# A Strassen-stepped attention block: first head pair by plain block products, last output block row by row, side transfers on another queue

## The chip, the cores and the metric

The kernel runs on one core of a Trainium2 chip. TensorE (PE) multiplies, VectorE (DVE) and ScalarE (ACT) work on tiles in SBUF and PSUM, GpSimd (POOL) does small things, and SyncE (SP) issues most DMAs. Each engine works through its own list of instructions in order. The metric is the device time of one launch in microseconds, lower is better.

## The reference

One layer is computed (DEPTH is 1, so only the neighbourhood attention of the two mixers), on 512 tokens of width 2048:

```python
h = rms_norm(x, norm_pre)
q, k, v, z = split(h @ na_w_in, 4)            # 2048 -> 4 * 2048
o = neighbourhood_attention(q, k, v, na_rpb)  # 16 heads of 128, 8 x 16 windows on an 8 x 64 grid
y = (o * silu(z)) @ na_w_out                  # 2048 -> 2048
out = x + rms_norm(y, norm_post)
```

The norm of a row of `h` is a factor per token, so the kernel multiplies the unnormalised `x` (scaled by the gain of each column) with the weights and applies the factor `rc` to the product.

## The kernel before, in words

**Products.** Every float32 operand is cut into a high part (`hi`, rounded to the fast matmul type by a CAST on ACT) and the rest (`lo`, a subtraction on DVE); a product is then three matmuls, hi by hi, lo by hi and hi by lo. One matmul is 128 x 128 by 128 x 512.

**Input steps.** The input product runs in `NSTEP` = 8 steps, one for each pair of heads. A step multiplies a 512 x 2048 activation with 2048 x 1024 weights. Both are cut in two along each dimension (blocks A11 to A22, B11 to B22), and a Strassen-Winograd scheme with seven block products (`NPASS`) replaces the eight plain ones. A pass is `KH` = 8 slots of k, a slot six matmuls (`mm_in`), so a step is 56 slots (`SLOTS`), 336 matmuls. The passes need sums of blocks. Sums of weights are made in the running tiles `T` on DVE (line 209) from `T` and a raw tile; sums of the activation are the same in all steps, are made once in the first step (`prep_a`, lines 129 to 151: A11, S1, A12, N2, A22, N4, N3), cut into hi and lo, and kept in SBUF as tiles `a`. So in the first step ACT and DVE have, beside the weights' work, the scaling of `x` by the gain (line 121), the sums (137 to 148) and the cuts (126, 127), one operand a slot. `combine` adds the passes' results into the four quadrants of the product.

**Beside the first step.** `square_x` loads `x` again in token order, 16 tiles `sq` of 256 KB in two alternating buffers, and ACT squares and sums them (line 166). After the last, `rstd` makes `rc` (DVE twice, then `pow` on POOL, line 171). Mask and squares are placed by slot number (`at`).

**Look-ahead.** `prep(m)` cuts the weights of slot m two slots ahead of the matmuls (`AHEAD`); `hi` and `lo` have three buffers each, raw weights four (`NRAW`). A framework lays tiles out in the pools, sets the waits, and sets the final order in each engine's list, close to the order of the code.

**Heads.** While step s runs, the attention of step s-1's two heads is laid beside its slots by the table `HEAD`. `load_bias` loads a head's position table, `keep_g` writes its gated output to DRAM (`graw`), `fetch_g`/`split_g` read it back (`gr`) and cut it into hi and lo (lines 486, 487) in the space of `a` tiles no longer used. All of these DMAs are issued on SP's list, between the loads of weights.

**Output.** Four blocks n of 512 output columns, each 16 slots of k; a slot multiplies four row tiles t of 128 tokens, twelve matmuls (`mm_out`). In each block the last two slots run tile by tile, so `finish(n, t)` can begin on tile 0 while PE is on tile 1. For the last block `finish` squares and sums (ACT, line 589), forms the row's norm (DVE 594, POOL 595), multiplies by the gain (DVE 596), scales four quarter rows and adds `x` (three on DVE, line 604; one on ACT and POOL, 601 and 602), and writes them out (606). `load_res` loads the residual tiles `xres`.

## Time and profile before

| | |
|---|---|
| median of 3 runs | 933.33 us (931.19 to 935.33) |
| the profiled execution | 932.95 us |
| its span, first to last instruction | 931.2 us |
| PE busy | 885.5 us, 95% |
| DVE, ACT busy | 730.5 us, 557.9 us |
| DMA | 180.1 MB, 193 GB/s over the span |

Times inside the profile count from the start of the span; the execution is 1.75 us longer than its span. PE's busy time counts overlapping matmuls whose ends are modelled, so a busy PE may still run below its pace; the pace is read from the distance of their starts. The times at which each step's first matmul starts cut the span into stages.

### The profile page before, as it was taken

The page shows a single profiled execution, that of the slowest core. Times are in us where ns is not written, and L with a number is a line of the kernel's source. Part 1 is how long each engine was busy: PE and PEld are TensorE (multiplying, and loading weights), DVE is VectorE, ACT ScalarE, POOL GpSimd, SP SyncE. Part 2 cuts the span into 40 slices and gives each one's busy share as a digit, 9 for nine tenths or more (in the row PEclk, how much of TensorE's full clock was granted, in tenths as well). Part 3 has the DMA queues.
Part 4 walks back from the last instruction along what each step waited for, and adds up shares of the span by engine and source line. Part 5 has one row for each costly group of instructions (what it writes and reads, how often), then busy time and mean ns, then how long its engine had stood idle before and what let it go on. Part 6 is the DMA issues. An engine that isn't in the chain of part 4 may idle for free.

```text
span 931.2 us, 13211 instructions
## 1 busy us (share of the span) xinstructions
PE 885.5 (95%) x4176; PEld 726.3 (78%) x4176; DVE 730.5 (78%) x1370; ACT 557.9 (60%) x1119; POOL 12.3 (1%) x18
## 2 busy tenths in 40 slices
PE   7887999999999999999999999999989999999992
PEld 6565788888788888888888888788868778888882
DVE  6997989897989799899979897989799654232326
ACT  8985675575658575766675575658566563232322
POOL 0000000000000000000000000000000000000003
PEclk9999999999999999999999999999999999999997
DMA  9798657865684678377656765685589922333325
GB/s 311 218 282 260 178 156 226 253 196 157 209 258 151 207 222 255 110 230 227 218 140 219 243 206 155 207 267 179 173 254 306 266 81 86 95 101 92 101 58 181
DMA packets 101734, 180.11 MB, mean 193 GB/s; under 512 B 11552, under 2 KB 17696, under 8 KB 101664
## 3 DMA queue, kind: packets, MB, share of 16 engines
q1 hardware_dynamic: 101232, 178.75, 62.6%
q8 instruction: 32, 0.52, 0.2%
q10 hardware_dynamic: 432, 0.53, 0.2%
q14 instruction: 38, 0.31, 0.1%
HBM read 171.37 MB, written 7.86 MB: 192 GB/s over the span
## 4 chain that ended last, share of the span: by engine, by line
issue 89%; DMA 5%; DVE 2%; ACT 1%; POOL 1%; PE 1%; SPq 0%; DVEq 0%; POOLq 0%; ACTq 0%
DMA sq<-in_x 2%; DMA x<-in_xT 1%; DMA raw<-in_w_in 1%; DVE lo L214 1%; PE u0Y L243 1%; POOL xres L602 1%; DVE a L127 1%; ACT hi L213 1%; DVE t L209 0%; DVE xres L604 0%; POOL rc L171 0%; ACT yg L601 0%; POOL rcy L595 0%; DVE x L141 0%; ACT a L126 0%
## 5 line engine op out<-in xcount | busy, mean ns | idle before, releaser
L213 ACT CAST hi<-t 128x512 fp32r<-128x512 f32 x320 | 196.1, 617 | 119.7 <-DVE t L209 25.0
L214 DVE TENSOR_TENSOR lo<-raw,hi 128x512 fp32r<-128x512 f32 x192 | 131.2, 690 | 135.3 <-ACT hi L213 129.0
L214 DVE TENSOR_TENSOR lo<-t,hi 128x512 fp32r<-128x512 f32 x320 | 217.4, 685 | 16.5 <-ACT hi L213 14.8
L213 ACT CAST hi<-raw 128x512 fp32r<-128x512 f32 x192 | 118.7, 621 | 152.6 <-PE y L583 93.3
L209 DVE TENSOR_TENSOR t<-t,raw 128x512 f32<-128x512 f32 x256 | 171.8, 686 | 14.3 <-DMA raw<-in_w_in 13.2
L583 PE MATMUL y<-hi,g 128*128 128x512 f32 x512 | 159.3, 392 | 0.4 <-DVE e L291 0.4
L583 PEld LDWEIGHTS y<-hi,g 128*128 128x128 f32 x512 | 95.1, 188 | 21.2 <-DVE e L291 0.9
L583 PE MATMUL y<-lo,g 128*128 128x512 f32 x256 | 99.7, 390 | 0.0
L583 PEld LDWEIGHTS y<-lo,g 128*128 128x128 f32 x256 | 48.1, 188 | 9.9
L243 PE MATMUL u0Y<-hi,a 128*128 128x512 f32 x96 | 27.8, 401 | 5.0 <-ACT a L126 2.6
L369 DVE TENSOR_TENSOR bm<-braw,mask_sb 128x256 f32<-128x256 f32 x48 | 27.2, 597 | 0.0
L243 PE MATMUL u1Y<-hi,a 128*128 128x512 f32 x96 | 26.8, 396 | 0.0
L243 PE MATMUL u2Y<-hi,a 128*128 128x512 f32 x96 | 26.8, 396 | 0.0
L243 PE MATMUL u3Y<-hi,a 128*128 128x512 f32 x96 | 26.8, 396 | 0.0
L243 PE MATMUL u4Y<-hi,a 128*128 128x512 f32 x96 | 26.8, 396 | 0.0
L243 PE MATMUL u6Y<-hi,a 128*128 128x512 f32 x96 | 26.8, 396 | 0.0
L243 PE MATMUL u5Y<-hi,a 128*128 128x512 f32 x96 | 26.8, 396 | 0.0
L243 PE MATMUL u7Y<-hi,a 128*128 128x512 f32 x96 | 26.8, 395 | 0.0
L298 ACT ACTIVATE s<-s,rc 128x512 f32<-128x512 f32 x32 | 22.9, 719 | 6.2 <-DVE s L283 5.7
L243 PE MATMUL u0X<-hi,a 128*128 128x512 f32 x64 | 19.7, 427 | 7.2 <-ACT hi L213 7.2
L243 PEld LDWEIGHTS u0Y<-hi,a 128*128 128x128 f32 x96 | 17.1, 188 | 12.0 <-ACT a L126 3.6
L243 PE MATMUL u0Z<-hi,a 128*128 128x512 f32 x64 | 18.4, 407 | 6.9 <-ACT hi L213 6.8
(405 smaller groups left out, 1858.5 us busy)
## 6 DMA issues: line engine op xcount, KB each, us to landing
raw<-in_w_in SPq DMA_DIRECT2D x384, 256.0 KB, 3.5
t<-in_w_in SPq DMA_DIRECT2D x128, 256.0 KB, 3.2
raw<-in_w_out SPq DMA_DIRECT2D x64, 256.0 KB, 2.6
x<-in_xT SPq DMA_DIRECT2D x32, 128.0 KB, 3.9
xres<-in_x SPq DMA_DIRECT2D x16, 256.0 KB, 6.9
graw<-zm SPq DMA_DIRECT2D x14, 256.0 KB
gr<-graw SPq DMA_DIRECT2D x14, 256.0 KB, 3.9
out<-xres SPq DMA_DIRECT2D x14, 256.0 KB, 3.0
```

Source lines behind the costliest of these rows:

```text
L127: nc.vector.tensor_tensor(lo, src, hi.bitcast(F32), ALU.subtract)
L209: nc.vector.tensor_tensor(T[k], T[k], src, ALU.add)
L213: nc.scalar.copy(hi, src)
L214: nc.vector.tensor_tensor(lo, src, hi.bitcast(F32), ALU.subtract)
L243: nc.tensor.matmul(U[c][s], l, r, start=p in (0, 1, 4) and k == 0 and s not in seen, stop=k == KH - 1 and n in (2, 5), skip_group_check=True,)
L298: nc.scalar.activation(t[:, s, :], t[:, s, :], AF.Copy, scale=rc[:, j + s : j + s + 1])
L369: nc.vector.tensor_tensor(bm[:, i, :].rearrange("p (a b) -> p a b", b=8), rev, mask_sb[:, i, :].unsqueeze(2).to_broadcast([P, 32, 8]), ALU ...
L583: nc.tensor.matmul(Y[n][t], l[:, tsl], r, start=k == 0 and i == 0, stop=k == KT - 1 and i == 2)
L602: nc.gpsimd.tensor_tensor(r, yg[q, t], r, ALU.add)
```

## The change

**First step.** Its seven passes become two (n = 0, 1) of 16 slots each (`FIRST` = 32 slots). Pass n forms one column half of the product by the plain sum over k: in a slot, four row tiles by one weight tile, twelve matmuls (`mm_first`), into four PSUM banks. No sums of weights are made, no `combine`; `take_first` copies the banks out with `rc` applied, for pass 0 from slot 22 on, for pass 1 at the end. An x tile is loaded whole (256 KB instead of two halves), scaled whole and cut whole (`take_x`): A11 and A12 go to their own place, A21 and A22 for now to the places of N4 and beside A12. The sums for later steps (`sum_x`) and their cuts lie at slots 12 to 25. The squares come one in every slot of twelve matmuls from slot 2 (before: one in every second slot of six, from slot 10), `rstd` at slot 20.

**Side transfers.** Mask, `load_bias`, `keep_g` and `fetch_g` are issued from GpSimd's list. The fetches move: heads 0 to 7 from slot 30 of the last input step, every third slot, into the space of A12 and A22; heads 8 to 13 one a slot from the first output slot. The residual tiles lie in the space of N2 and N3.

**Last block.** The last `TAIL` = 6 slots of the last block run tile by tile instead of 2; their weight cuts get buffers of their own (`w_tiles`). The last block's `y` lies in `T`.

```diff
+FIRST = 2 * KT
+TAIL = 6
...
+    AT = {}
+    for k in range(KH):
+        for n, ops in enumerate(((A11, N4, S1), (A12, A22), (N2, N3))):
+            t = ag.tile([P, len(ops), 2, 256], F32R, tag=f"a{k}_{n}", name=f"a{k}_{n}")
+            for i, o in enumerate(ops):
+                AT[k, o] = (t, i)
+
+    def A(k, o):
+        t, i = AT[k, o]
+        return t[:, i]
...
+    def load_x(k):
+        kk = k % KH
+        if k >= KH:
+            X[k] = small("v" if kk < 4 else "z", f"x{k}")
+        elif kk < 4:
+            X[k] = small("qk", f"x{k}")
+        else:
+            if kk % 2 == 0:
+                X["c", kk] = pair(f"x{k}")
+            X[k] = X["c", kk - kk % 2][:, kk % 2, :]
+        nc.sync.dma_start(X[k], xT[k])
+
+    def split_a(k, src, o):
+
+        t, i = AT[k, o]
+        src = src.rearrange("p (a b) -> p a b", b=256)
+        hi, lo = t[:, i : i + 2, 0, :], t[:, i : i + 2, 1, :]
         nc.scalar.copy(hi, src)
         nc.vector.tensor_tensor(lo, src, hi.bitcast(F32), ALU.subtract)
 
-    def prep_a(o, k):
-        x0, x1 = (X.get(k), X.get(k + KH))
+    def take_x(k):
+        nc.scalar.activation(X[k], X[k], AF.Copy, scale=gcol[:, k : k + 1])
+        split_a(k % KH, X[k], A11 if k < KH else A12)
...
+    def sum_x(k):
+        nc.vector.tensor_tensor(x1[:, h1], x0[:, h1], x1[:, h1], ALU.subtract)
+        nc.vector.tensor_tensor(x0[:, h1], x0[:, h0], x0[:, h1], ALU.subtract)
+        nc.vector.tensor_tensor(x0[:, h0], x0[:, h0], x1[:, h1], ALU.subtract)
+        nc.vector.tensor_tensor(x1[:, h0], x1[:, h0], x0[:, h0], ALU.subtract)
...
-    NIN = NSTEP * SLOTS
+    NIN = FIRST + (NSTEP - 1) * SLOTS
     NOUT = 4 * KT
     N = NIN + NOUT
 
+    def base(step):
+        return FIRST + (step - 1) * SLOTS if step else 0
...
+    def w_tiles(m):
+        if m < N - TAIL:
+            return tuple(wp.tile([P, L], F32R, tag=t, name=f"{t}{m}") for t in ("hi", "lo"))
+        i = m - N + TAIL
+        return tuple(small(("qk", "v", "z")[i // 2], f"{t}{m}", F32R) for t in ("hi", "lo"))
+
     def prep(m):
-        if m < NIN:
-            step, p, k = where(m)
-            if step == 0:
-                prep_a(p, k)
+        sums = FIRST <= m < NIN and where(m)[1] in (1, 3, 4, 6)
+        if m < FIRST and where(m)[1] == 0:
+            take_x(m)
...
+            if p == 1 and k >= KH:
+                load_t(1, B11, k - KH)
...
+    def mm_first(m):
+        _, n, k = where(m)
+        if k == 0:
+            if n == 0:
+                U[n] = [pm.tile([P, L], F32, tag=f"u{j}", name=f"u0_{j}") for j in range(4)]
+            else:
+                U[n] = [px.tile([P, L], F32, tag="ST"[j // 2], name=f"u1_{j}") for j in range(4)]
+        hi, lo = W.pop(m)
+        kk = k % KH
+        a = (A(kk, A11), A(kk, N4)) if k < KH else (A(kk, A12), A(kk, A22))
+        ops = [
+            (a[j // 2][:, i, j % 2 * P : j % 2 * P + P], w, j, i2)
+            for i2, (i, w) in enumerate(((0, hi), (1, hi), (0, lo)))
+            for j in range(4)
+        ]
+        if k == KT - 1:
+            ops.sort(key=lambda op: op[2])
+        for l, r, j, i in ops:
+            nc.tensor.matmul(U[n][j], l, r, start=k == 0 and i == 0, stop=k == KT - 1 and i == 2)
+
+    def take_first(n, j):
+        c = C.setdefault(0, {})
+        name = ("11", "12", "21", "22")[n + j // 2 * 2]
+        if j % 2 == 0:
+            c[name] = pair(f"c{name}_0")
+        nc.scalar.activation(c[name][:, j % 2, :], U[n][j], AF.Copy, scale=rc[:, j : j + 1])
...
-        nc.sync.dma_start(raw[:, 0 : 7 * TBL + 32], src)
+        nc.gpsimd.dma_start(raw[:, 0 : 7 * TBL + 32], src)
...
-            nc.sync.dma_start(graw[h], z_of[h])
+            nc.gpsimd.dma_start(graw[h], z_of[h])
...
-            nc.sync.dma_start(g, graw[h])
+            nc.gpsimd.dma_start(g, graw[h])
...
+            t = ag.tile([P, 2, L], F32R, tag=f"a{k}_{1 - o}", name=f"g{h}")
...
-            m = NIN - SLOTS + 17 + 3 * h if h < HEADS - 4 else NIN + h - HEADS + 4
+            m, wait = (NIN - SLOTS + 30 + 3 * h, 4) if h < KH else (NIN + h - KH, 3)
             at(m, fetch_g, h)
-            at(m + 4, lambda h=h: done.pop(h)())
+            at(m + wait, lambda h=h: done.pop(h)())
...
-        at(10 + 2 * i, begin)
-        at(14 + 2 * i, lambda i=i: pending.pop(i)())
-    at(45, rstd)
-    at(40, lambda: nc.sync.dma_start(mask_sb, mask))
+        at(2 + i, begin, i)
+        at(4 + i, lambda i=i: pending.pop(i)())
+    at(8, lambda: nc.gpsimd.dma_start(mask_sb, mask))
+    at(20, rstd)
+    for j in range(4):
+        at(22 + j, take_first, 0, j)
+        at(FIRST - 1, take_first, 1, j)
+    for k in range(KH):
+        at(KT - 4 + k, sum_x, k)
+        at(KT - 3 + k, lambda k=k: split_a(k, X[k], N2))
+        at(KT + 1 + k, lambda k=k: split_a(k, X[k + KH], N4))
...
+            free[k] = ag.tile([P, 2, L], F32, tag=f"a{k}_2", name=f"spare{k}")
...
-        y = yg[n, t] = spare(16 + n * 4 + t, f"yg{n}_{t}") if n < 2 else pair_half(n * 4 + t)
+        y = yg[n, t] = pair_half(n * 4 + t) if n < 3 else T[4 + t]
...
+        if 0 <= m and m + 3 < KT:
+            load_x(m + 3)
...
+            last = TAIL if n == 3 else 2
+            if k < KT - last:
                 mm_out(m, range(4))
             elif k == KT - 1:
                 for t in range(4):
-                    mm_out(m - 1, [t])
-                    mm_out(m, [t])
+                    for mm in range(m - last + 1, m + 1):
+                        mm_out(mm, [t])
                     finish(n, t)
```

**ACT, first step.** Names: `sq` the squares' tiles, `hi` weights, `a` and `x` the activation, `c` a copy out of PSUM. Before, around the fifth square:

```order
L166 ACTIVATE sq_548,part<-sq_548 128x512
L213 CAST hi_625<-raw_559 128x512
L126 CAST a_3_150<-x_190 128x256
L126 CAST a_3_157<-x_190 128x256
L126 CAST a_4_123<-x_257 128x256
L126 CAST a_4_130<-x_275 128x256
L166 ACTIVATE sq_584,part<-sq_584 128x512
L213 CAST hi_641<-t_161 128x512
```

and now, in the first pass, around the sixth:

```order
L164 ACTIVATE sq_351,part<-sq_351 128x512
L140 ACTIVATE x_362<-x_362,gcol 128x512
L164 ACTIVATE sq_377,part<-sq_377 128x512
L136 CAST a_1_112<-x_362 128x2x256
L227 CAST hi_382<-raw_281 128x512
L140 ACTIVATE x_388<-x_388,gcol 128x512
L164 ACTIVATE sq_403,part<-sq_403 128x512
L136 CAST a_1_115<-x_388 128x2x256
L227 CAST hi_409<-raw_307 128x512
```

A slot now has a scaling, a cut of `x`, a cut of a weight and a square, in that company four ACT instructions of 512 columns for twelve matmuls. Where the scale factor arrives, after the last square, ACT now has:

```order
L164 ACTIVATE sq_621,part<-sq_621 128x512
L164 ACTIVATE sq_648,part<-sq_648 128x512
L227 CAST hi_598<-raw_491 128x512
L271 ACTIVATE c_0_776<-u_0_184,rc 128x512
L271 ACTIVATE c_0_776<-u_1_185,rc 128x512
L227 CAST hi_629<-raw_521 128x512
```

Here `hi_598` is the weight of slot 18 and `hi_629` that of slot 19, which now stands behind two copies that read `rc`.

**SP and POOL, last input step.** Before, on SP (`gr` a fetched head, `xres` a residual tile, `t` and `raw` weights):

```order
L100 DMA t_163<-in_w_in 128x512
L610 DMA xres_0_8901<-in_x 128x1x512
L478 DMA gr_7643<-graw 128x512
L100 DMA t_164<-in_w_in 128x512
L478 DMA gr_7694<-graw 128x512
L100 DMA t_165<-in_w_in 128x512
L610 DMA xres_1_8903<-in_x 128x1x512
L100 DMA t_166<-in_w_in 128x512
L198 DMA raw_7651<-in_w_in 128x512
L198 DMA raw_7672<-in_w_in 128x512
L100 DMA t_167<-in_w_in 128x512
```

Now SP has only weights there, and POOL's list holds the fetches, a bias table and the write of head 13:

```order
L514 DMA gr_7521<-graw 128x512
L514 DMA gr_7586<-graw 128x512
L514 DMA gr_7633<-graw 128x512
L514 DMA gr_7726<-graw 128x512
L504 DMA graw<-zm_7222 128x512
L399 DMA braw_7945<-in_rpb 128x1x368
L514 DMA gr_7780<-graw 128x512
L514 DMA gr_7823<-graw 128x512
L514 DMA gr_7853<-graw 128x512
L514 DMA gr_7884<-graw 128x512
```

The fetches no longer stand between weights; nine are ahead of the write of head 13, five behind it.

**PE, last block.** Before, the two last slots (`hi_9397`, `hi_9413`) by tiles `y_0`, `y_1`, after `y_3` of the slot ahead:

```order
L583 MATMUL y_3_9189<-lo_9382,g_0_8200 128x512
L583 MATMUL y_0_9186<-hi_9397,g_0_8266 128x512
L583 MATMUL y_0_9186<-hi_9397,g_1_8267 128x512
L583 MATMUL y_0_9186<-lo_9398,g_0_8266 128x512
L583 MATMUL y_0_9186<-hi_9413,g_0_8486 128x512
L583 MATMUL y_0_9186<-hi_9413,g_1_8487 128x512
L583 MATMUL y_0_9186<-lo_9414,g_0_8486 128x512
L583 MATMUL y_1_9187<-hi_9397,g_0_8266 128x512
```

and now, six slots:

```order
L629 MATMUL y_3_8898<-lo_9021,g_7881 128x512
L629 MATMUL y_0_8895<-hi_9038,g_7913 128x512 x2
L629 MATMUL y_0_8895<-lo_9039,g_7913 128x512
L629 MATMUL y_0_8895<-hi_9056,g_7948 128x512 x2
L629 MATMUL y_0_8895<-lo_9057,g_7948 128x512
L629 MATMUL y_0_8895<-hi_9074,g_7983 128x512 x2
L629 MATMUL y_0_8895<-lo_9075,g_7983 128x512
L629 MATMUL y_0_8895<-hi_9078,g_8044 128x512 x2
L629 MATMUL y_0_8895<-lo_9079,g_8044 128x512
L629 MATMUL y_0_8895<-hi_9082,g_7986 128x512 x2
L629 MATMUL y_0_8895<-hi_9086,g_8208 128x512 x2
L629 MATMUL y_1_8896<-hi_9038,g_7913 128x512 x2
```

Between the last matmul of one row tile and that of the next there are now 18 matmuls instead of 6; the number of matmuls is the same.

## Rows read from the trace of the kernel before

**Rows 1.** Busy time by stretch: first pass of the first step, its rest, the fourth step, the last input step, the output blocks, the end. Columns: stretch in us, its length, busy us (instructions) of PE, PEld, DVE, ACT, POOL, granted clock of PE as a share, share of DMA time, GB/s.

```profile
0.00:20.10 20.10, 15.39 (x64) 13.02 (x65) 12.40 (x24) 16.44 (x36) 0.91 (x9) 1.00 0.92 309
20.10:107.00 86.90, 72.59 (x294) 52.15 (x294) 80.30 (x168) 65.86 (x157) 2.26 (x1) 1.00 0.87 253
281.90:368.70 86.80, 86.80 (x425) 72.72 (x424) 78.06 (x146) 57.02 (x111) 0.00 (x0) 1.00 0.67 210
631.50:725.70 94.20, 89.29 (x426) 72.11 (x425) 83.51 (x157) 62.63 (x123) 0.00 (x0) 1.00 0.74 228
725.70:914.10 188.40, 186.36 (x857) 153.04 (x855) 73.56 (x138) 68.41 (x141) 2.23 (x2) 1.00 0.36 103
914.10:931.20 17.10, 0.00 (x0) 0.00 (x0) 12.04 (x16) 2.74 (x5) 6.92 (x7) 0.62 0.77 241
```

**Rows 2.** The matmul line's groups (ns min/median/max of one, first and last start in us): the first chain of steps 0 and 1, and the output product.

```profile
L243 PE MATMUL u0X<-hi,a x64: 387/389/796, 4.7 to 47.7; 128*128 128x512 f32 x64
L243 PE MATMUL u1X<-hi,a x64: 387/393/477, 107.0 to 142.7; 128*128 128x512 f32 x64
L583 PE MATMUL y<-hi,g x512: 387/389/499, 725.7 to 913.4; 128*128 128x512 f32 x171
```

**Rows 3.** Timeline of PE (start us, us, what): two successive slots of six matmuls at full pace, and the warm-up products in the first step with the matmul behind them.

```profile
159.90 1.07 PE L243 MATMUL u1Z<-hi,a 128*128 128x512 f32 x4
161.26 1.07 PE L243 MATMUL u1Z<-hi,a 128*128 128x512 f32 x4
...
8.71 2.72 PE L83 MATMUL warm<-ident 128*128 128x128 f32 x16
11.19 0.48 PE L243 MATMUL u0X<-hi,a 128*128 128x512 f32 x1
```

**Rows 4.** Groups by line of the first 110 us, ACT and then DVE: busy us, mean ns of one, idle before.

```profile
L213 ACT CAST hi<-t 128x512 fp32r<-128x512 f32 x44 | 26.8, 615 | 10.7 <-DVE t L209 5.8 <-PE u0Z L243 2.4 <-PE u0X L243 0.9
L126 ACT CAST a<-x 128x256 fp32r<-128x256 f32 x48 | 18.1, 400 | 0.7 <-DVE x L148 0.3
L121 ACT ACTIVATE x<-x,gcol 128x256 f32<-128x256 f32 x32 | 15.6, 505 | 0.7 <-DMA gcol<-in_gpre 0.7
L166 ACT ACTIVATE sq<-sq 128x512 f32<-128x512 f32 x16 | 10.1, 631 | 4.7 <-DMA sq<-in_x 4.5
L166 ACT ACTIVATION_READ_ACCUMULATOR sq<-sq 128x1 f32 x16 | 3.0, 186 | 0.0
L298 ACT ACTIVATE s<-s,rc 128x512 f32<-128x512 f32 x4 | 2.9, 719 | 0.7 <-DVE s L283 0.7
...
L209 DVE TENSOR_TENSOR t<-t,raw 128x512 f32<-128x512 f32 x32 | 21.9, 686 | 0.5 <-DMA raw<-in_w_in 0.4
L127 DVE TENSOR_TENSOR a<-x,a 128x256 fp32r<-128x256 f32 x48 | 19.5, 421 | 5.9 <-ACT a L126 5.9
```

**Rows 5.** DMA: the mean rate in 10 to 20 us, then, of 49.3 to 63 us, the mean rate and the issues of the squares' tiles (KB each, median us from issue to landing); the same row of the whole page; and ACT's timeline of two successive squares, with the idle time before each and what ended it.

```profile
DMA packets 3036, 3.66 MB, mean 366 GB/s; under 512 B 335, under 2 KB 2160, under 8 KB 3036
...
DMA packets 2164, 3.94 MB, mean 288 GB/s; under 512 B 239, under 2 KB 239, under 8 KB 2164
sq<-in_x SPq DMA_DIRECT2D x5, 256.0 KB, 4.4
...
sq<-in_x SPq DMA_DIRECT2D x12, 256.0 KB, 5.6
...
58.90 0.63 ACT L166 ACTIVATE sq<-sq 128x512 f32<-128x512 f32 x1 [0.16 <-DMA sq<-in_x]
61.46 0.63 ACT L166 ACTIVATE sq<-sq 128x512 f32<-128x512 f32 x1 [0.19 <-DMA sq<-in_x]
```

**Rows 6.** Timeline where the row factor `rc` is made and first used.

```profile
88.89 2.26 POOL L171 TENSOR_TENSOR rc<-ms,mhalf 128x4 f32<-128x4 f32 x1 [87.43 <-DVE ms L170]
...
91.19 0.72 ACT L298 ACTIVATE c<-c,rc 128x512 f32<-128x512 f32 x1 [3.44 <-POOL rc L171]
```

**Rows 7.** Timeline of the end: the first row tile's square, the last matmul, the starts of row tiles 2 and 3 on DVE, and DVE's last group (three instructions).

```profile
910.02 0.60 ACT L589 ACTIVATE yg<-y 128x512 f32<-128x512 f32 x1 [3.68 <-PE y L583]
911.61 3.11 DVE L604 SCALAR_TENSOR_TENSOR xres<-yg,rcy,xres 128x512 f32<-128x512 f32 x3
913.68 0.39 PE L583 MATMUL y<-lo,g 128*128 128x512 f32 x1
918.51 0.20 DVE L594 TENSOR_SCALAR msy<-part,ms 128x1 f32<-128x1 f32 x1
922.38 0.20 DVE L594 TENSOR_SCALAR msy<-part,ms 128x1 f32<-128x1 f32 x1
923.24 3.08 DVE L604 SCALAR_TENSOR_TENSOR xres<-yg,rcy,xres 128x512 f32<-128x512 f32 x3
```

**Rows 8.** The last input step, 631.5 to 725.7 us: what ACT's cut of the fetched heads waited for (us in total, times, longest), and the DMA issues (KB each, median us to landing).

```profile
ACT g L486 <- DMA gr<-graw: 8.1, 9, 1.8
...
gr<-graw SPq DMA_DIRECT2D x13, 256.0 KB, 3.9
...
xres<-in_x SPq DMA_DIRECT2D x6, 256.0 KB, 7.3
```

**Rows 9.** Two lines' instructions (ns min/median/max): DVE's scale-and-add of the end, two inputs from SBUF, and POOL's addition that runs beside some of them.

```profile
L604 DVE SCALAR_TENSOR_TENSOR xres<-yg,rcy,xres x12: 744/752/1776, 911.6 to 924.6; 128x512 f32<-128x512 f32 x12
...
L602 POOL TENSOR_TENSOR xres<-yg,xres x4: 1737/1737/1759, 912.4 to 924.0; 128x512 f32<-128x512 f32 x4
```

129 lines of the change are left out of this document (43 added, 86 removed).

## The prediction

> **What bounds the kernel now.** I read the stretches first, to see where PE is busy but not at its pace. In a middle step PE is busy for all of 86.80 us [rows 1], so this stage is PE's own time. Its pace is read from the starts of two slots: 1.36 us for six matmuls, 0.2267 us each [rows 3]. A step of 336 matmuls is 76.2 us, and two heads' attention the other 10.6 us. Held against this, three stages are too long. The first step starts at 4.7 us and the second at 107.0 us [rows 2]: 102.3 us for 76.2 us of products and 2.5 us of warm-up products (8.71 to 11.19) [rows 3], so 23.6 us are lost. In its long part DVE is busy 80.30 us of 86.90 [rows 1]: sums and cuts of both operands. The last input step takes 94.2 us, 7.4 more than a middle one. The output has 768 matmuls (174.1 us) and two heads (10.6 us) in 188.4 us [rows 1], 3.7 us lost. And from the last matmul, which ends at 914.1 us, to the end at 931.2 us PE does nothing: 17.1 us [rows 1].
>
> **First step.** Two passes of 16 slots of twelve matmuls are 384, or 87.0 us, 10.9 us more than now. What goes is DVE's 32 sums of weights (21.9 us [rows 4]), the passes' combinations, and 24 of the 56 weight cuts on each engine. Then:
> - Start. The first x tile is 256 KB instead of 128 (0.36 us more at 366 GB/s [rows 5]), its scaling about 0.72 instead of 0.51 us, its cut 0.62 instead of 0.40 [rows 4]: the first matmul comes at 4.7 + 0.8 = 5.5 us.
> - The warm-up products remain, 2.5 us. The first pass of before had 48 products (10.9 us) and the warm-up between 4.7 and 20.1 us, so 2.0 us went at the start [rows 1 to 3]; I leave them in.
> - Without another stall the step ends at 5.5 + 87.0 + 2.5 + 2.0 = 97.0 us, against 107.0.
>
> Now the stalls X. In the first pass a slot asks ACT for a scaling (0.72), a cut of x (0.62), a weight's cut (0.62) and a square (0.63 + 0.19) [rows 4]: 2.78 us, against 2.72 us of PE. That is a tie. By the new order eleven squares and five cuts for later steps stand ahead of the pass's last weight on ACT, so its total is 16 x 1.96 + 11 x 0.82 + 5 x 0.62 = 43.5 us; PE's is 43.5. DVE needs 1.38 us a slot, and from slot 12 up to 3.7 us (three cuts of 0.69, four sums of 0.42 [rows 4]); the two slots of look-ahead (5.4 us) cover the eight slots in which this is over PE's pace. DMA has to bring x, weight and square, 786 KB a slot, 289 GB/s; 288 GB/s were reached in the stretch with squares and 366 without them [rows 5]. So that is a tie as well. The squares are a chain: a buffer's load takes 4.4 us to land in that stretch, 0.82 us to be squared and about 0.3 us to be issued anew, so two squares in 5.5 us; two of before stand 2.56 us apart, with ACT waiting for each [rows 5]. Sixteen squares then need as much as their slots. Behind the last one come two small DVE operations, POOL's 2.26 us for `rc`, and two copies of 0.72 us [rows 4, 6], and only then ACT cuts the weight of slot 19: 4 us, with PE at most two slots off. ACT has waited here before (3.44 us [rows 6]), for less.
>
> I take X = 3 us. Its ends: 0, if ACT's lead of two slots covers all, and 10, if a square's load takes 5.6 us as over the whole trace [rows 5]: then two squares take 6.7 us, 0.63 us a slot over PE, sixteen times. The second pass has nothing like it (no x, last squares), and is at PE's pace. The step ends at 100.0 us: **7.0 us gained**, between 0 and 10.
>
> **Last block.** Row tile 0's chain of before runs from ACT's square at 910.02 us to the end of DVE's adds at 914.72: 4.7 us. The other tiles queue behind it on DVE, 3.87 us apart (918.51, 922.38), and DVE ends at 926.32, 4.84 us before the end [rows 7]. Now 18 matmuls, 4.08 us, lie between two tiles, more than DVE's 3.87, so no queue forms and the last tile takes 4.7 + 4.84 = 9.5 us after the last matmul instead of 17.1. What hides the first three tiles is PE's work on the next; the number of matmuls is the same. The weights of the six slots must be cut before PE reaches them: they have their own buffers and wait for no matmul, and PE has three slots (8.2 us) ahead of them. **7.5 us gained**, between 6 and 8.
>
> **Side transfers.** In the last input step ACT waited 8.1 us, nine times, for a fetched head, and 13 fetches and 6 residual tiles were issued there [rows 8]. Now nine fetches remain, none stands between weights on SP, and the residual tiles cannot come before the last pass. All 11.1 us of excess in this step and the output may not go: four of thirteen fetches are 2.3 us of the 7.4, and I add 0.7 for the weights that no longer queue. **3 us gained.** Upper end 8, if weights' loads were the cause of most. Lower end -5: how long a POOL-issued transfer takes, the trace does not show; the nearest row is 3.9 us from SP, and if the nine land 1 us later each, ACT waits 9 us more, of which by before's ratio (7.4 of excess with 8.1 of waiting) nearly all could reach PE; I take half, since some cover is left. The bias tables have no such risk: their buffer is free a head ahead, and POOL has nothing else to do.
>
> Making transfers on POOL may cost DVE. Of DVE's scale-and-adds at the end most take 0.75 us, but beside POOL's addition of 1.74 us up to 1.78 [rows 9]: 1.0 us more. I take nothing for it. If each of the 45 transfers (16 tables, 14 writes, 14 fetches, the mask) did the same, that would be four a step, 4.1 us, and DVE is idle for 8.7 us of a middle step (86.80 less 78.06 [rows 1]). The Trainium skill, page "GPSIMD Engine Reference", Specifications, says that GpSimd's SBUF interface is shared with VectorE and contended by instructions with two SBUF inputs; the rows agree. Page "DMA: Bandwidth & Descriptors", SWDGE vs HWDGE vs iDMA, adds that GpSimd writes its descriptors into SBUF, which transfers from SyncE never do, and so speaks against this part of the change; no run so far shows it. By it the sum would lose something in every step, by the trace alone nothing.
>
> **Sum.** 7.0 + 7.5 + 3 = 17.5 us off the profiled execution's 932.95 us, which is 0.4 us below the median: **915.5 us**.
>
> **Rivals.**
> - *Everything covered.* X = 0 and most of the excess of the last step gone: 10 + 7.5 + 8, so 907.5 us. For it: two squares of before follow each other in 2.56 us, less than a slot [rows 5]. Against it: three ties at once in the first pass.
> - *The first pass starves.* X = 10: 922.5 us. For it: 5.6 us to land; the factor's chain blocks ACT in order.
> - *The stalls only change their place.* The first step has 10.9 us more of products, and if the passes lose 20 us as they do now, the step ends at 117 us and the rest just pays for it: 932.5 us. Against it: DVE's load, the cause, falls by half.
> - *POOL's transfers hold DVE (slower than before).* The place is every step: four transfers, each holding DVE's two-input operations. From (8.7 + 3.2) / 4 = 3.0 us each it costs all that is gained and 5 us more, over seven steps. At 3.2 us each it is 4.1 us a step, 28.7 us, so 944 us. For it: rows 9's mechanism. Against it: that row gives 1.0 us for an operation on a whole tile, and a transfer's bookkeeping is not one.
>
> **How the numbers follow.** Forecast 915.5 us (910 to 920): 0.55. Covered, 907.5: 0.15. Starved, 922.5: 0.15. Stalls moved, 932.5: 0.08. POOL holds DVE, 944: 0.07. Leaving out the last two and a little of the fastest gives 907 to 925. A change of 0.5%, about 4.7 us, is what a measurement here can tell from none. The first three cases are faster: 0.85; the fourth is the same: 0.08; the last slower: 0.07.
>
> **What would show it.** The second step's first matmul near 100 us (97 to 107), with slots of 2.72 us apart from a gap near slot 19 ended by ACT. From the last matmul to the end about 9.5 us, DVE idle between row tiles. The last input step near 91 us. DVE's two-input operations still 0.69 us in the middle steps, these still 86.8 us. I am wrong if the first pass's slots stand over 3.3 us apart, if the last block waits for cuts of its six weights, or if the middle steps grow.

## The result and the profile after

The changed kernel takes **922.21 us** (median, 920.21 to 924.74) against 932.26 us before (930.63 to 935.33); the ratio is **0.989**, interval 0.985 to 0.993. That is 10.1 us less, where 915.5 us were forecast, 17.5 less; the range (907 to 925) and the side held. The profiled execution took 921.92 us, with a span of 920.1 us.

The stretches of the changed kernel, cut where the same stages begin and end as in [rows 1]: start of the first step, its rest, all six middle steps, the last input step, the output, the end, and the fourth step alone. Columns as in [rows 1].

```profile
0.00:24.40 24.40, 18.66 (x78) 15.83 (x79) 9.84 (x15) 16.28 (x28) 1.61 (x10) 1.00 0.72 235
24.40:102.60 78.20, 74.59 (x324) 60.12 (x323) 47.51 (x90) 47.45 (x94) 2.39 (x3) 1.00 0.66 191
102.60:624.70 522.10, 521.67 (x2546) 436.29 (x2546) 463.59 (x867) 338.49 (x660) 13.00 (x24) 1.00 0.66 203
624.70:717.90 93.20, 88.41 (x425) 72.50 (x424) 82.28 (x153) 60.88 (x119) 8.20 (x15) 1.00 0.69 213
717.90:910.70 192.80, 188.93 (x857) 155.37 (x855) 83.28 (x151) 72.43 (x147) 8.49 (x9) 0.98 0.42 120
910.70:920.10 9.40, 0.00 (x0) 0.00 (x0) 4.53 (x6) 1.41 (x3) 2.38 (x3) 0.61 0.70 220
277.20:364.00 86.80, 86.80 (x426) 72.72 (x425) 77.79 (x146) 56.73 (x111) 2.16 (x4) 1.00 0.67 206
```

The matmul lines' groups that answer to [rows 2]: first and last start are the last two times of a row.

```profile
L264 PE MATMUL u<-hi,a x256: 387/389/794, 5.7 to 102.2; 128*128 128x512 f32 x128
L285 PE MATMUL u1X<-hi,a x64: 389/389/486, 102.6 to 138.7; 128*128 128x512 f32 x64
L629 PE MATMUL y<-hi,g x512: 387/389/628, 717.9 to 910.1; 128*128 128x512 f32 x171
```

Held against [rows 1, 2], stage by stage: the second step starts at 102.6 instead of 107.0 us, 4.4 gained. The middle steps take 522.1 instead of 524.5 us, 2.4 gained; other kernels here whose middle steps are written alike lie between 521.8 and 525.5, so this is scatter between executions. The last input step takes 93.2 instead of 94.2, 1.0 gained. The output takes **192.8 instead of 188.4, 4.4 lost**. The end takes 9.4 instead of 17.1, 7.7 gained. The sum is 11.1 us of span.

Each stage is read from one execution, and the experiments' kernels show how far one execution can be off where the code of a stage is the same. With the change's own code the first step ends at 101.4 (e1) to 102.6 us, the last input step takes 92.1 (e2) to 93.7 us (e11), and the output 190.7 (e11) to 194.3 us (e9). So the output's loss against 188.4 lies between 2.3 and 5.9 us; of the kernel before there is one profile only.

**The first step.** PE's timeline where its pace breaks (start us, us, what, idle time before and what ended it):

```profile
58.73 2.12 PE L264 MATMUL u<-hi,a 128*128 128x512 f32 x8 [1.00 <-ACT hi L227]
60.69 1.08 PE L264 MATMUL u<-lo,a 128*128 128x512 f32 x4
63.70 2.14 PE L264 MATMUL u<-hi,a 128*128 128x512 f32 x8 [1.93 <-ACT hi L227]
67.13 1.20 PE L264 MATMUL u<-hi,a 128*128 128x512 f32 x4 [0.38 <-ACT hi L227]
```

ACT in the same stretch, parts of its list in order:

```profile
60.41 0.63 ACT L164 ACTIVATE sq<-sq 128x512 f32<-128x512 f32 x1 [1.21 <-DMA sq<-in_x]
...
62.41 0.63 ACT L164 ACTIVATE sq<-sq 128x512 f32<-128x512 f32 x1 [1.28 <-DMA sq<-in_x]
...
63.04 0.60 ACT L227 CAST hi<-raw 128x512 fp32r<-128x512 f32 x1
65.30 1.27 ACT L271 ACTIVATE c<-u,rc 128x512 f32<-128x512 f32 x2 [1.66 <-POOL rc L169]
66.46 0.62 ACT L227 CAST hi<-raw 128x512 fp32r<-128x512 f32 x1
```

POOL's timeline at 63 to 66 us, and SP's (its DMA issues) at 43 to 46 us:

```profile
63.44 0.55 POOL L399 DMA_DIRECT2D braw<-in_rpb  x1 [61.21 <-DMA t<-in_w_in]
64.00 1.26 POOL L169 TENSOR_TENSOR rc<-ms,mhalf 128x4 f32<-128x4 f32 x1
```

```profile
43.53 0.54 SPq L163 DMA_DIRECT2D sq<-in_x  x1
44.13 0.58 SPq L114 DMA_DIRECT2D t<-in_w_in  x1
```

The reader is to see that PE waits for a weight's cut on ACT, and that ACT cuts it late because a square stands ahead of it in the list and waits for its own DMA; in the last case two of the four scalings (L271) that need `rc` stand ahead. Against the 2.72 us of a slot, the slot that starts at 63.70 comes 2.25 us late after the one at 58.73 (a square stands ahead of its weight), the slot at 67.13 only another 0.71 us (the scalings). Beside the squares SP issues loads of `T` (L114), operands of the second step, from 44 us on. POOL issues the bias table, now on its queue, just ahead of `rc`. That costs `rc` little: from the end of the DVE operation ahead of it (63.54 us) to its own end it takes 1.72 us here; of the four runs that issue the bias table from SP again, three take as long (1.71 to 1.72 us in e3, e8 and e14) and one takes 1.19 (e12).

The step's end is worked out as 5.7 (first matmul) + 87.0 + 4.6 (the first seven matmuls start at 5.74 us and the warm-up at 8.89, 1.56 us more than seven times 0.2267; the products go on at 11.90, 3.01 us later) = 97.3; the other 5.3 us are stalls.

**The start of the output.** PE's timeline around its longest wait:

```profile
725.07 0.39 PE L629 MATMUL y<-hi,g 128*128 128x512 f32 x1
729.31 0.58 PE L422 MATMUL s<-k14h,q14h 128*128 128x256 f32 x1 [3.84 <-ACT q14h L364]
```

Windows of 2 us over the same place; the granted clock is the number after POOL's:

```profile
725.90:727.90 2.00, 0.00 (x0) 0.00 (x0) 0.91 (x2) 0.36 (x2) 0.00 (x0) 1.00 1.05 277
727.90:729.90 2.00, 0.59 (x2) 0.54 (x3) 1.60 (x3) 1.35 (x3) 0.00 (x0) 0.63 1.06 262
729.90:731.90 2.00, 2.00 (x10) 1.90 (x10) 0.29 (x1) 1.10 (x3) 0.00 (x0) 0.50 1.08 254
```

ACT's timeline, its two late cuts:

```profile
724.87 0.62 ACT L227 CAST hi<-raw 128x512 fp32r<-128x512 f32 x1 [3.63 <-DMA raw<-in_w_out]
727.65 0.62 ACT L227 CAST hi<-raw 128x512 fp32r<-128x512 f32 x1 [1.64 <-DMA raw<-in_w_out]
```

PE is idle for 3.84 us, and then runs at the lower of its two levels (0.50, 1.2 GHz). ACT waits for weights of the output (L207) and, as it works in order, cuts the operand q14h (of head 14's attention) late; the DMA share is over 1. The DMA issues of the last input step, beside [rows 8]: now eight residual loads (`spare`), and the output's weights, issued between them, take 9.7 us to land.

```profile
gr<-graw POOLq DMA_DIRECT2D x11, 256.0 KB, 4.0
...
spare<-in_x SPq DMA_DIRECT2D x8, 256.0 KB, 6.8
raw<-in_w_out SPq DMA_DIRECT2D x4, 256.0 KB, 9.7
```

SP's timeline, the first and the last group of the sixteen residual loads:

```profile
707.08 0.55 SPq L656 DMA_DIRECT2D spare<-in_x  x1
...
729.70 2.35 SPq L656 DMA_DIRECT2D spare<-in_x  x3
```

They are issued within 26 us, so SP does not have only weights in the last input step: eight residual loads come in its last 11 us, eight more in the output's first 14. In the kernel before the same sixteen were issued from 689.24 to 738.8 us, but only two of them early, at 689.24 and 692.83; the other fourteen came within 24 us, four in the last 11 us before its output starts (725.7), ten in the 13 us behind:

```profile
692.83 0.55 SPq L610 DMA_DIRECT2D xres<-in_x  x1
...
714.59 0.55 SPq L610 DMA_DIRECT2D xres<-in_x  x1
...
736.64 2.17 SPq L610 DMA_DIRECT2D xres<-in_x  x3
```

So the crowd at the start of the output is not new. In the kernel before it left PE idle for 2.04 us in all of the output, at a clock of 1.00 (188.40 less 186.36 [rows 1]); now it is 3.84 us in one piece, and the clock falls behind it.

**The end.** DVE's timeline of the last two row tiles, as in [rows 7]: they start 4.07 us apart, and DVE stands still for some 0.1 us between them, so the 18 matmuls are only just enough. The operation beside POOL's addition is the long one again, as in [rows 9].

```profile
907.36 0.21 DVE L640 TENSOR_SCALAR msy<-part,ms 128x1 f32<-128x1 f32 x1
...
911.43 0.21 DVE L640 TENSOR_SCALAR msy<-part,ms 128x1 f32<-128x1 f32 x1
...
912.31 1.42 DVE L650 SCALAR_TENSOR_TENSOR spare<-yg,rcy,spare 128x512 f32<-128x512 f32 x2
913.64 1.75 DVE L650 SCALAR_TENSOR_TENSOR spare<-t,rcy,spare 128x512 f32<-128x512 f32 x1
```

### The profile page after: what moved, and what is told of

The parts are those of the page before. It is cut to its first block, busy times and chain, and to the rows that moved or that the text cites. A ratio compares the mean times of both kernels' runs of the same rounds, so it can differ in the third digit from the quotient of the medians.

```text
span 920.1 us, 13073 instructions
## 1 busy us (share of the span) xinstructions
PE 892.3 (97%) x4224; PEld 740.1 (80%) x4224; DVE 691.0 (75%) x1279; ACT 536.9 (58%) x1049; POOL 36.1 (4%) x63
## 4 chain that ended last, share of the span: by engine, by line
PE 65%; issue 21%; DMA 7%; DVE 3%; ACT 1%; POOL 1%; SPq 0%; DVEq 0%; POOLq 0%; ACTq 0%
PE u L264 4%; PE u6Y L285 4%; PE u3Y L285 4%; PE u2Y L285 4%; PE u5Y L285 4%; PE u4Y L285 4%; PE u1Y L285 3%; DMA raw<-in_w_in 3%; PE u5Z L285 2%; PE u3X L285 2%; PE u1X L285 2%; PE u2X L285 2%; PE u6X L285 2%; PE u5X L285 2%; PE u4X L285 2%
## 5 line engine op out<-in xcount | busy, mean ns | idle before, releaser
L228 DVE TENSOR_TENSOR lo<-raw,hi 128x512 fp32r<-128x512 f32 x208 | 142.2, 690 | 159.4 <-ACT hi L227 136.5
L227 ACT CAST hi<-t 128x512 fp32r<-128x512 f32 x280 | 171.0, 618 | 111.7 <-DVE t L224 30.1
L227 ACT CAST hi<-raw 128x512 fp32r<-128x512 f32 x208 | 128.0, 621 | 161.5 <-PE y L629 79.1
L228 DVE TENSOR_TENSOR lo<-t,hi 128x512 fp32r<-128x512 f32 x280 | 189.9, 684 | 12.1 <-ACT hi L227 8.4
L224 DVE TENSOR_TENSOR t<-t,raw 128x512 f32<-128x512 f32 x224 | 150.1, 686 | 10.6 <-DMA raw<-in_w_in 9.6
L264 PE MATMUL u<-hi,a 128*128 128x512 f32 x256 | 66.7, 399 | 9.1 <-ACT hi L227 9.0
L264 PEld LDWEIGHTS u<-hi,a 128*128 128x128 f32 x256 | 48.6, 191 | 20.7 <-ACT hi L227 10.8
L264 PE MATMUL u<-lo,a 128*128 128x512 f32 x128 | 35.3, 390 | 0.2 <-DVE lo L228 0.2
L137 DVE TENSOR_TENSOR a<-x,a 128x512 fp32r<-128x512 f32 x32 | 21.7, 687 | 11.7 <-ACT a L136 11.5
L264 PEld LDWEIGHTS u<-lo,a 128*128 128x128 f32 x128 | 24.0, 188 | 5.7 <-DVE lo L228 0.7
```

The source lines that it names most:

```text
L137: nc.vector.tensor_tensor(lo, src, hi.bitcast(F32), ALU.subtract)
L224: nc.vector.tensor_tensor(T[k], T[k], src, ALU.add)
L227: nc.scalar.copy(hi, src)
L228: nc.vector.tensor_tensor(lo, src, hi.bitcast(F32), ALU.subtract)
L264: nc.tensor.matmul(U[n][j], l, r, start=k == 0 and i == 0, stop=k == KT - 1 and i == 2)
```

## The experiments

The theory after the result: the last block gains what was forecast; the output's loss comes of the 16 residual loads, which now all fall into 26 us around the start of the output; the first step's stalls come of the squares and the factor `rc` ahead of weights on ACT. The rivals are named with each run. Times are medians beside runs of the kernel before on the same chip (931.6 to 932.4 us); ratios are to these. The stages are those of each kernel's one profiled execution; the output ends with the end of the last matmul.

### Residual loads held (e1)

`xres` may be loaded as soon as its space is free, after the last pass. A one-column copy from a tile of output block 1 into it holds the load until that tile is there.

```diff
+        nc.gpsimd.tensor_copy(xres[t, q][:, 0:1], yg[1, t][:, 0:1])
         nc.sync.dma_start(xres[t, q], x_v[...])
```

> The changed kernel with one edit: a residual tile's first column is first written by POOL from the second output block's result, so its load cannot start before that block is done. Theory (the sixteen residual loads, now all at the start of the output, crowd out the output weights there; PE runs dry for 3.8 us, and its granted clock then stands at half for some 6 us): the output stage falls from 192.8 to 185 to 187 us, the granted clock stays at 1.00 there, the time falls by 6 to 7 us to about 915.5 us. Rival (the fetches of heads issued from POOL come late at the start of the output): they are not touched, the stage stays above 191 us, the time within 1 us of the changed kernel.

Measured: 915.63 us, ratio 0.983 (0.980 to 0.985). The output takes 186.0 us. Its window up to the last matmul's start, 0.4 us before its end:

```profile
716.10:901.70 185.60, 185.60 (x856) 153.12 (x855) 82.72 (x151) 72.35 (x147) 11.07 (x25) 1.00 0.45 125
```

PE is busy for all of the output and the clock stays at 1.00: the wait and the fallen clock are both gone. The residual loads were their cause. The weights show it: in the first 19 us of the output they land in 2.7 us here and in 8.6 in the change. 6.8 us of the 192.8 belong to the residual, more than the 4.4 lost, so the kernel before paid some as well. The traces of the other runs agree: the six with the change's residual loads and fetches (the change, e2, e4, e9, e11, e13) all have PE waiting for q14h at this place, 2.64 to 5.88 us, with the lower clock beside or behind it and an output of 190.5 to 194.3 us; the four in which the loads are held (e1, e8, e12, e14) have neither, and take 186.0 to 186.8.

### The same in the kernel before (e7)

> The kernel before with its residual loads held until a tile of the second output block is there, nothing else. Theory: the loads crowd the start of the output there too, in part; the output takes 185 to 186 us instead of 188.4 and the last input step 92 to 93 instead of 94.2, together 928. Rival: with 6 of 16 loads already out of the way before, the rest collides with nothing; then 932 as before.

Measured: 927.14 us, ratio 0.996 (0.994 to 0.997); the output 186.0 instead of 188.4, the last input step 90.9 instead of 94.2. So the kernel before did have the same loss, in a milder form: of its 11.1 us of excess in these two stages, 5.7 were the residual's (4.5 by the medians).

### Side transfers back on SP's queue (e3)

```diff
-        nc.gpsimd.dma_start(...)    # bias table, graw, gr, mask
+        nc.sync.dma_start(...)
```

> The changed kernel with mask, bias tables, writes and fetches of heads issued from SyncE again, at the slots of the change. Theory (the move gives a little: side transfers that wait on SyncE hold the weights behind them): steps 1 to 6 together take 524 to 525 us instead of 522.1, with the excess in the third and the seventh step that the kernel before had, the last input step above 94 us, the time 2 to 4 us above the changed kernel, about 925 us. Rival (GpSimd's transfers slow DVE or come later): the middle steps get shorter, the last input step and the output too, the time 2 us or more below. Second rival (worth nothing): within 1 us.

Measured: 916.95 us, ratio 0.985 (0.982 to 0.987), some 5 us faster than the change. The theory that the move helps fell. In its profiled execution (919.41 us, the slowest of its four) the last input step takes 90.9 us instead of 93.2 and the output 191.3 instead of 192.8, while the first step and the middle ones take 1.5 us more; so the profile places only half of the 5 us, and of its parts only the 2.3 us of the last input step lie outside the scatter of one stage. Its DMA issues of the last input step:

```profile
gr<-graw SPq DMA_DIRECT2D x9, 256.0 KB, 3.6
...
spare<-in_x SPq DMA_DIRECT2D x5, 256.0 KB, 6.8
raw<-in_w_out SPq DMA_DIRECT2D x5, 256.0 KB, 6.3
```

On SP nine fetches and five residual loads fall into this step, on GpSimd's queue eleven and eight; the output's weights land in 6.3 instead of 9.7 us, and ACT's cut of the fetched heads waits 2.3 us (three times) instead of 5.6 (five times). A fetch does not take longer on GpSimd's queue (median 4.5 us over the whole execution with either). On SP the residual loads also spread over 706.24 to 740.8 us instead of 707.08 to 732. So SP's queue held fetches and residual back behind weights, and on the whole that was worth more than the places which the fetches took among the weights. At the start of the output another wait takes the place of the change's: PE stands still for 2.90 us, and ACT waits 6.4 us for a fetched head and not for weights.

### Both (e8)

> The changed kernel with the residual's loads held until a tile of the second output block is there, and the side transfers back on SP's queue. Theory: the two gains lie in different stages; the move to GpSimd costs 2.3 us in the last input step (93.2 against 90.9), the residual 7.4 in the output (192.8 against 185.4). Together 913, the last input step 90.5 to 91, the output 185 to 186. Rival: both relieve the same transfers around the start of the output; then it is the 915.6 of the held loads alone, with a last input step of 92.

Measured: 914.01 us, ratio 0.980 (0.978 to 0.982), last input step 89.6, output 186.8. The gains add in the last input step (91.9 to 89.6) and not in the output. By the totals e8 cannot be told from e1 (0.983, 0.980 to 0.985); by the stage, the 2.3 us appear both times (93.2 to 90.9 as well).

### The last block with two slots held back (e4)

```diff
-TAIL = 6
+TAIL = 2
```

> The changed kernel with the last block's tile-by-tile part set back from six slots to two. Theory (row tiles queue on DVE when PE delivers them every 1.4 us): from the last matmul to the end 17.1 us instead of 9.4, the time 7.7 us above the changed kernel, about 930 us. Rival (part of the gain is from buffers and not from the spacing): 12 to 14 us from the last matmul, the time 3 to 5 us above.

Measured: 929.97 us, ratio 0.998 (0.996 to 1.000). From the last matmul to the end it takes 16.6 us instead of 9.4, and 7.8 us are lost in all. So the last block alone is worth most of what the change gives; the other parts together give some 2 us.

### The first step as before (e5)

The kernel before with the last block's and the side transfers' parts of the change alone, the operand tiles as before.

```diff
+TAIL = 6
+    (w_tiles and the last block's loop as in the change)
-        nc.sync.dma_start(...)      # bias table, graw, gr, mask
+        nc.gpsimd.dma_start(...)
-            m = NIN - SLOTS + 17 + 3 * h if h < HEADS - 4 else NIN + h - HEADS + 4
+            m, wait = (NIN - SLOTS + 30 + 3 * h, 4) if h < KH else (NIN + h - KH, 3)
```

> The kernel before with two parts of the change, side transfers on GpSimd's queue with the new places of the fetches, and the last block tile by tile; the first step by Strassen's passes and the operand tiles as before, so 6 of 16 residual tiles come already in the last input step. Theory: the output's loss of 4.4 us comes of the new operand tiles, which free all 16 residual tiles only with the last pass. Then the output takes 188 to 189 us here, the first step 107, the tail 9.5, and the time is 922 to 924. Rival: the output's loss comes of GpSimd's queue or of the last block; then the output takes 192.8 here as well and the time is about 926.5.

Measured: 924.31 us, ratio 0.992 (0.990 to 0.995). First step 107.7, last input step 97.4, output 186.7, end 9.5. With the old operand tiles, and the residual loads issued from 685.20 to 730.7 us, the output has no loss on GpSimd's queue, so the rival falls. The loss moved, though: 15 of the 16 residual loads now fall into the last input step (6 before, 8 in the change), which is 3.2 us longer than before. ACT waits there 10.2 us for fetched heads instead of 8.1, and behind one of these waits PE stands still for 1.92 us and then runs at 0.50 from 701 to 704 us. How much of the 3.2 us is the residual's and how much GpSimd's queue's, this run does not part. Against this run the change's first step is worth some 3 us in all (0.992 against 0.989, with intervals that overlap).

### Four runs on the first step's stalls (e2, e9, e11, e13)

Squares on four tiles (`T` 4 to 7, which are free) instead of two buffers, finished three slots after their load (e2); these, spread over slots 2 to 24 (e9); `T`'s loads held until the weight of their slot is cut (e11); the four scalings held until the weight of their slot is cut (e13).

```diff
-        t = sp.tile([P, L], F32, tag=("bm", "braw")[i % 2], name=f"sq{i}")
+        t = T[4 + i % 4]                                          # e2, e9
...
-        at(2 + i, begin, i)
+        at(2 + 3 * i // 2, begin, i)                              # e9
...
-    at(20, rstd)
+    at(27, rstd)                                                  # e9; 21 in e2
...
-        at(22 + j, take_first, 0, j)
+        at(30 - j // 2, take_first, 0, j)                         # e9; 23 + j in e2
...
+                nc.gpsimd.tensor_copy(T[k - KH][:, 0:1], hi.bitcast(F32)[:, 0:1])                  # e11
                 load_t(1, B11, k - KH)
...
+            nc.gpsimd.tensor_copy(c[name][:, j % 2, 0:1], W[24 + j][0].bitcast(F32)[:, 0:1])       # e13
         nc.scalar.activation(c[name][:, j % 2, :], U[n][j], AF.Copy, scale=rc[:, j : j + 1])
```

> The changed kernel with the squares' tiles in four buffers (weight tiles that are idle then) instead of two, each squared one slot later, and the row factor one slot later. Theory (a square's load is issued only when the buffer's last square is done, so two buffers make a chain a little slower than a slot, which ends at slots 16 to 20 in PE's stalls of 5.0 us): the waits of ACT for squares (10.1 us) mostly go, the second step starts at 97.5 to 99 us instead of 102.6, the time falls by 4 us to about 918 us. Rival (ACT is full, or DMA is): waits move to weights or x, the second step starts at 101.5 to 103 us, the time within 1 us.

> The changed kernel with the sixteen squares on four buffers of their own, begun over slots 2 to 24 instead of 2 to 17, the root after slot 27 and the first head's four scalings at slots 29 and 30. Theory: what is left of the first step's stalls comes of 4 MB of squares loaded beside the input and the weights (the DMA share is 1.0 and more from 36 to 60 us) and of the scalings that stand in ScalarE's queue waiting for the root; then the step ends at 98 to 99 instead of 102.6 and the time is 918 to 919 where the change has 922.2. Rival one: ScalarE and VectorE are full with the casts and sums of the second pass; then the stalls move behind slot 16, the step ends at 102 and the time stays 922. Rival two: the later root delays the first products of the second step, which take over these banks; then the second step grows by 2 us.

> The changed kernel with the eight loads of the second step's operands (L114, 256 KB each, which SP issues from 44 to 62 us though the second step starts at 102.6) held until the weight is cast beside which they stand in the program, by an eight-fold one-column copy on GpSimd. Theory: these 2 MB are what the first step's squares, input and weights compete with from 36 to 60 us, where the DMA share is 1.0; without them the squares come in time and only the wait for the root stays: 5.5 + 87.0 of products + 4.6 of start + 1.7 = 98.8 instead of 102.6, and the time is 918 to 919 where the change has 922.2. Rival: input, squares and weights alone, 768 KB for each slot of 2.72 us or 289 GB/s, fill the DMA engines; then the step ends at 101.5 to 102.5 and the time stays at 921 to 923.

> The changed kernel with the first head's four scalings (L271) held, each by a one-column copy on GpSimd, until the weight is cast beside which it stands in the program (slots 22 to 25), so that they stand behind the casts of weights 18 to 24 in ScalarE's queue and not ahead of them. Theory: of the 5.1 us of stalls in the first step 2.1 and 0.55 are the scalings' wait for the root ahead of two weights; they go, the 1.7 us before stay: the step ends at 99.5 to 100.5 instead of 102.6 and the time is 919.5 to 920.5 where the change has 922.2. Rival: the weights behind wait for the last squares in any case, whose loads are late between the second step's operands; then the stall moves on by one slot, the step ends at 102 to 103, the time stays at 922.

Measured, against the change's 922.2 us and 102.6 us:

| run | time | ratio, interval | first step ends |
|---|---|---|---|
| e2, four tiles | 923.25 | 0.992 (0.989 to 0.994) | 102.2 |
| e9, squares spread | 923.87 | 0.992 (0.990 to 0.994) | 104.1 |
| e11, `T` held | 922.48 | 0.990 (0.988 to 0.993) | 102.5 |
| e13, scalings held | 922.96 | 0.990 (0.988 to 0.993) | 102.7 |

None gains. Each shortened the wait that it was made for and left PE waiting in the same place for what stood next (in e2 and e9 ACT waits 4.9 and 6.6 us for the squares' loads instead of 10.1, but still 2.3 and 1.6 us for `rc`). In e11 the DMA share of 54 to 66 us falls to 0.58 and 0.32, and the squares wait 5.7 us for their loads instead of 10.1, but the scalings still wait 1.67 us for `rc`. In e13 the scalings wait for no `rc`, and the casts stand behind squares that still come late: the last one is waited for 1.27 us, and PE stands still for 1.79.

In two of the four the clock hides what the edit did: behind their last stall it falls to 0.50, in e11 from 64 us and in e13 from 63 us on, while it stays at 1.00 in the change, e2 and e9. By the windows of 1 us this took 1.7 us of work from each. An estimate from these rows: without the fall the step would have ended at 100.8 us (e11) and 101.0 us (e13), so each of the two edits may have gained 1.6 to 1.8 us that the clock took back; one execution's scatter in this stage, 101.4 to 102.6, is nearly as large.

In e9 the order by slot number did not hold: the scalings, put at slots 29 and 30, run at 64.66 us, about slot 18, as soon as `rc` is there, and wait 1.63 us for it. So a late slot in the code did not keep an instruction back in its engine's list, while the copies of e11 and e13, on which it has to wait, did.

### Three and four edits together (e12, e14)

e12 is e8 with e11's edit, e14 is e12 with e13's.

> The changed kernel with three edits together: the residual's loads held for the second output block, the side transfers back on SP's queue, the second step's operands held as above. Theory: the edits lie in three stages and their gains add: 914 less 3.5 is 910.5, with the first step at 99 to 100, the last input step at 90 and the output at 186. Rival: the first step keeps its 103.8 of the run with both others, and the time stays at 914.

> The run with the three edits (residual held, side transfers on SP's queue, second step's operands held) with the scalings held as well. Theory: there all of the first step's stalls, 3.3 us at 62 and 1.5 us of a halved clock behind it, come of the scalings that wait for the root ahead of a weight; without them the step ends at 97.5 to 98.5 instead of 102.3 and the time is 908 to 909 instead of 912.4. Rival: the squares themselves stand ahead of the weights and are late; then the step ends at 101 to 102 and the time is 911 to 912.

Measured: e12 takes 912.39 us, ratio 0.979 (0.978 to 0.981), first step to 102.3; e14 takes **910.62 us, ratio 0.977** (0.974 to 0.979), first step to 100.3, the fastest here. PE's timeline of e12 and then of e14 at the place of the last stall (their L265 is the change's L264, e12's L272 its L271). e12:

```profile
58.55 1.07 PE L265 MATMUL u<-lo,a 128*128 128x512 f32 x4
62.75 3.45 PE L265 MATMUL u<-hi,a 128*128 128x512 f32 x8 [3.13 <-ACT hi L227]
```

and, of ACT in e12, the scaling ahead of that weight:

```profile
61.50 0.69 ACT L272 ACTIVATE c<-u,rc 128x512 f32<-128x512 f32 x1 [1.62 <-POOL rc L169]
```

e14:

```profile
59.55 1.07 PE L265 MATMUL u<-lo,a 128*128 128x512 f32 x4
61.16 2.12 PE L265 MATMUL u<-hi,a 128*128 128x512 f32 x8 [0.54 <-ACT hi L227]
...
66.67 1.20 PE L265 MATMUL u<-lo,a 128*128 128x512 f32 x4 [0.66 <-DVE lo L228]
```

With `T`'s loads out of the way and the scalings behind the weights, the stall of 3.13 us shrinks to 0.54: in e12 it was the scalings' wait. In the profiles the first step ends at 102.5 and 102.7 with one of the two edits alone, at 102.3 with `T`'s loads held on top of e8's 103.8, and at 100.3 with both. But e8, e11, e12 and e13 each lost 1.7 us there to the lower clock, and e14 lost none, having no idle time of 1 us left; so 1.7 of the 2.0 us between e12 and e14 are the clock's, and that both edits are needed is not shown. By the totals e14 and e12 cannot be told apart. Neither rival came true in full, nor did the 97.5 to 98.5 us of the theory: squares still stand ahead of weights (ACT waits 6.7 us for their loads in e14). That all four edits with e2's tiles would take the rest was not tried.

## Why the prediction came out as it did

**First step: right mechanism, mis-sized.** Forecast 7.0 us, measured 4.4. The products (87.0) and the start (5.7 + 4.6 against 5.5 + 4.5) were right. The term X was 3 and measured 5.3, inside its ends of 0 and 10. The chain was named: squares, then `rc`, then two copies ahead of a weight, and the gap was expected near slot 19, ended by ACT; the largest lies at 63.70 us, slot 18, ended by ACT. The shares were other, though: the copies ahead of slot 19 cost 0.7 us, and most came before them, of squares whose loads ACT waited for (10.1 us in all). One thing was not in the term: the sum of what DMA has to bring counted input, weight and square, not the 2 MB of `T`, which SP issues up to 50 us before their use. The runs e2 to e14 show more than one cause in a row on ACT's list, and a clock that falls behind some of the waits and not behind others, which takes 1.7 us each time and for which the prediction had no term. `T`'s loads and the scalings taken away together (e14) give 2.3 us of the 5.3. That the rest is the squares' is argued from ACT's waits, not tried alone.

**Last block: right.** Forecast 7.5 us, measured 7.7; e4 gives it by itself, 7.2 at the end and 7.8 in all. Row tiles are 4.07 us apart and no queue forms on DVE, with 0.1 us to spare.

**Side transfers, last input step and output: wrong.** Forecast 3 gained, measured 3.4 lost (1.0 gained and 4.4 lost). The step that failed is "none stands between weights on SP, and the residual tiles cannot come before the last pass", which was counted as relief. The second half is true and is most of the loss: the new operand tiles free the residual's space only with the last pass, so the 16 loads of 256 KB are issued in 26 us among the first weights of the output, eight of them still in the last input step, where six had been. e1 holds them and the output drops from 192.8 to 186.0 us; of that, 3.84 us are PE's wait, and some 3.4 us, by the windows, the lower clock behind it, which the prediction had no term for. Why nearly the same crowd, fourteen loads in 24 us, took less from the kernel before is not shown beyond this: there PE was idle for 2.04 us and the clock did not fall.

The first half costs too: e3 puts the transfers back between the weights and gains 5 us. The timetable of fewer fetches, which was to give 2.3, gave little: eleven were issued in this step, not nine, and on SP's queue, where it was nine, the last input step takes 90.9 us (e3) against 94.2 before, and with the residual held 89.6 (e8) against 90.9 (e7), 1.3 to 3.3 gained; but the output, into which the other five fall, gives most of it back. Over both stages it is 282.2 us (e3) against 282.6, and 276.4 (e8) against 276.9 (e7): 0.4 to 0.5 gained.

GpSimd's queue takes 2.3 back in the last input step and 1.5 over both stages (e1, 277.9, against e8), within the forecast's lower end, though not in the way that was thought: the fetches take no longer. The residual takes 8.1 us of both stages in the change (286.0 against e1's 277.9) and took 5.7 before. So, by these single executions, the timetable gained 0.5, GpSimd's queue lost 1.5 and the residual 2.4 more than before: the 3.4 us that were lost.

**DVE beside GpSimd's transfers: right at nothing.** The sums of weights take 686 ns on the mean over all 224, as in [rows 4], and the fourth step has 77.79 us of DVE against 78.06. The rule of the Trainium skill ("DMA: Bandwidth & Descriptors", SWDGE vs HWDGE vs iDMA) that GpSimd writes its descriptors into SBUF does not show as a price on DVE here. The Trainium skill's rule of the shared interface ("GPSIMD Engine Reference", Specifications) shows where POOL computes on whole tiles, as before: L650 takes 1.75 us beside POOL's addition, and two of them take 1.42 us together without.

**The rivals.** *Everything covered* (907.5 us) fell with the 5.3 us of stalls and the output's loss. *The first pass starves* gave 922.5 us, and the time is 922.2; but the first step ended at 102.6, not 107, and the same total came about by the output's loss. A total that hits a rival's number does not show its mechanism. *POOL's transfers hold DVE* is refuted by the fourth step. *The stalls only change their place* is refuted by the first step's end.

## What to carry to other kernels

When a change alters which buffers share space, list what else waits for that space and where its loads will now fall: a load that nobody needs for 100 us can delay the ones that are needed at once, and its price is read from the landing times of its neighbours on the queue. A transfer that is moved off a busy in-order queue loses its place behind urgent transfers as well as its wait; and before removing one wait, look at what stands behind it on the same engine's list, since removing one of several can give nothing. Where an edit seems to give nothing, read the granted clock of the stretch before calling it useless: here, by estimate, the clock took from two edits about as much as they had gained.

## What was not expected of the hardware

After an idle time of PE the granted clock can fall to 0.50 (1.2 GHz) when work has already resumed, and it stays there for some us of full work. In e11 PE stood still for 2.6 us, ran again from 62.71 us at full clock, and was given the lower level from 64 us to some time after 67 (windows of PE alone: its busy us and instructions, the granted clock, DMA share, GB/s):

```profile
63.00:64.00 1.00, 1.00 (x6) 1.00 0.00 0
64.00:65.00 1.00, 1.00 (x4) 0.56 0.46 78
65.00:66.00 1.00, 1.00 (x4) 0.50 0.48 184
66.00:67.00 1.00, 1.00 (x4) 0.50 0.57 75
```

The length of one idle time does not tell, in these traces, whether the clock falls. PE's timeline in the first step of e3 and of e9, eight matmuls each:

```profile
63.49 2.78 PE L264 MATMUL u<-hi,a 128*128 128x512 f32 x8 [1.82 <-ACT hi L227]
...
65.91 2.12 PE L264 MATMUL u<-hi,a 128*128 128x512 f32 x8 [1.87 <-ACT hi L227]
```

Behind 1.82 us in e3 the clock is at 0.50 from 65 to 68 us, behind 1.87 us in e9 it stays at 1.00. It fell as well behind 1.79 (e13), 1.92 (e5, last input step), 2.16 (e8), 2.60 (e11), 3.13 (e12) and 3.84 us (the change, output), and it did not behind 1.93 and 2.11 us (the change, first and last input step). By the windows of 1 us a fall in the first step took 1.7 us of work (e3, e8, e11, e12, e13), that in the change's output 3.4. So one stall of 3.84 us cost the output about 7 us: it took 192.8 with it and 186.0 without.
